# Rotary embedding, bf16 inside and f32 outside: smaller transfers with loads and stores taking turns in the software DMA queue

## The chip, the cores and the metric

The kernel runs on one core of a Trainium2 chip. Times are device microseconds (us) of one launch, as the median of several runs. "Span" is the length of one profiled execution; the time of the launch is a little above it.

## The reference

```python
# x: (8, 8, 1024, 64) f32; freqs: (32,) f32; positions: (1024,) int
angles = np.outer(positions, freqs)
cos, sin = np.cos(angles), np.sin(angles)
x_first, x_second = x[..., :32], x[..., 32:]
out_first  = x_first * cos - x_second * sin
out_second = x_first * sin + x_second * cos
```

16.78 MB are read and 16.78 MB written, both in f32. Each element takes part in three operations of the vector engine (DVE), which is little for so much data.

## The kernel before

A tile is 128 partitions, each with C = 64 positions of one head: 64 x 64 f32, a run of 16 KB in memory. Eight tiles cover x. All eight loads are issued by POOL (the GpSimd engine) at the start. They cast f32 to bf16 on the way, so a tile holds 8 KB per partition; the stores cast back (the packet records of this kernel hold 1024 load packets of 8 KB and 1024 store packets of 16 KB). ("Software queue" is below the queue that POOL fills, q0 software_dynamic in the page's rows; SP fills q1 and ACT q10, both hardware_dynamic.)

```python
C = 64; chunks = seq // C; group = P // chunks; ntiles = bh // group; run = C * d
pos_i = singles.tile([P, C, 1], positions.dtype)
for g in range(group):                       # 8 small DMAs on SP and ACT in turn
    eng = nc.sync if g % 2 == 0 else nc.scalar
    eng.dma_start(out=pos_i[g * chunks:(g + 1) * chunks],
                  in_=bass.AP(tensor=positions.tensor, offset=positions.offset,
                              ap=[[C, chunks], [1, C], [1, 1]]))
fr = singles.tile([P, half], f32)
nc.scalar.dma_start(out=fr, in_=freqs[None, :].to_broadcast([P, half]))
for g in range(ntiles):                      # all loads first
    xt = xpool.tile([P, C, d], bf16)
    nc.gpsimd.dma_start(out=xt.rearrange("p c d -> p (c d)"), in_=hbm(x, g))
    xts.append(xt)
# ... cut: tables sin_h, cos_h of [P, C, half] in bf16, by three DVE passes and three on ACT ...
for g in range(ntiles):
    # ... cut: views xf, xs of xt and of, os_ of ot; temporaries t1, t2 ...
    v.tensor_mul(out=t1, in0=xf, in1=sin_h)
    v.tensor_mul(out=t2, in0=xs, in1=sin_h)
    v.tensor_mul(out=of, in0=xf, in1=cos_h)
    v.tensor_mul(out=os_, in0=xs, in1=cos_h)
    v.tensor_sub(out=of, in0=of, in1=t2)
    v.tensor_add(out=os_, in0=os_, in1=t1)
    nc.gpsimd.dma_start(out=hbm(out, g), in_=ot.rearrange("p c d -> p (c d)"))
```

Of the kernel before, what the change touches and what calls it, by code (L numbers as in the profile page):

```python
# [2 lines left out]

# [4 lines left out]


@with_exitstack  # L10
def kernel(
    ctx: ExitStack,
    tc: tile.TileContext,
    x: bass.AP,
    freqs: bass.AP,
    positions: bass.AP,
    out: bass.AP,
):
    nc = tc.nc
    f32 = mybir.dt.float32  # L20
    bf16 = mybir.dt.bfloat16
    Sin = mybir.ActivationFunctionType.Sin
    Alu = mybir.AluOpType

    b, h, seq, d = x.shape
    bh = b * h
    half = d // 2
    P = 128
    twopi = 2 * math.pi


    C = 64
    chunks = seq // C
    group = P // chunks
    ntiles = bh // group
    run = C * d
    assert chunks * C == seq and group * chunks == P and ntiles * group == bh

    singles = ctx.enter_context(tc.tile_pool(name="singles", bufs=1))
    xpool = ctx.enter_context(tc.tile_pool(name="xin", bufs=ntiles))  # L40
    opool = ctx.enter_context(tc.tile_pool(name="xout", bufs=ntiles))
    tpool = ctx.enter_context(tc.tile_pool(name="tmp", bufs=2))

    def hbm(t, g):
        return bass.AP(tensor=t.tensor, offset=t.offset + g * P * run, ap=[[run, P], [1, run]])


    pos_i = singles.tile([P, C, 1], positions.dtype)
    for g in range(group):
        eng = nc.sync if g % 2 == 0 else nc.scalar  # L50
        eng.dma_start(
            out=pos_i[g * chunks:(g + 1) * chunks],
            in_=bass.AP(tensor=positions.tensor, offset=positions.offset,
                        ap=[[C, chunks], [1, C], [1, 1]]))
    fr = singles.tile([P, half], f32)
    nc.scalar.dma_start(out=fr, in_=freqs[None, :].to_broadcast([P, half]))


    xts = []
    for g in range(ntiles):  # L60
        xt = xpool.tile([P, C, d], bf16)
        nc.gpsimd.dma_start(out=xt.rearrange("p c d -> p (c d)"), in_=hbm(x, g))  # L62
        xts.append(xt)


    half_pi = singles.tile([P, 1], f32)
    nc.vector.memset(half_pi, math.pi / 2)  # L67
    pos_f = singles.tile([P, C, 1], f32)
    nc.vector.tensor_copy(out=pos_f, in_=pos_i.bitcast(mybir.dt.int32)[:, :, :1])  # L69
    fturn = singles.tile([P, 1, half], f32)  # L70
    nc.vector.tensor_scalar_mul(out=fturn[:, 0, :], in0=fr, scalar1=1.0 / twopi)  # L71
    turns = singles.tile([P, C, half], f32)
    nc.vector.tensor_mul(out=turns, in0=pos_f.to_broadcast([P, C, half]),  # L73
                         in1=fturn.to_broadcast([P, C, half]))
    whole = singles.tile([P, C, half], f32)
    magic = 1.5 * 2.0 ** 23
    nc.vector.tensor_scalar(out=whole, in0=turns, scalar1=magic, scalar2=magic,  # L77
                            op0=Alu.add, op1=Alu.subtract)
    nc.vector.tensor_sub(out=turns, in0=turns, in1=whole)  # L79
    sin_h = singles.tile([P, C, half], bf16)  # L80
    cos_h = singles.tile([P, C, half], bf16)
    nc.scalar.activation(out=sin_h, in_=turns, func=Sin, scale=twopi)  # L82

    nc.scalar.activation(out=whole, in_=turns, func=mybir.ActivationFunctionType.Abs)  # L84
    nc.scalar.activation(out=cos_h, in_=whole, func=Sin, scale=-twopi, bias=half_pi)  # L85

    v = nc.vector
    for g in range(ntiles):
        xt = xts[g]
        xf = xt[:, :, :half]  # L90
        xs = xt[:, :, half:]
        ot = opool.tile([P, C, d], bf16)
        of = ot[:, :, :half]
        os_ = ot[:, :, half:]
        t1 = tpool.tile([P, C, half], bf16)
        t2 = tpool.tile([P, C, half], bf16)
        v.tensor_mul(out=t1, in0=xf, in1=sin_h)  # L97
        v.tensor_mul(out=t2, in0=xs, in1=sin_h)  # L98
        v.tensor_mul(out=of, in0=xf, in1=cos_h)  # L99
        v.tensor_mul(out=os_, in0=xs, in1=cos_h)  # L100
        v.tensor_sub(out=of, in0=of, in1=t2)  # L101
        v.tensor_add(out=os_, in0=os_, in1=t1)  # L102
        nc.gpsimd.dma_start(out=hbm(out, g), in_=ot.rearrange("p c d -> p (c d)"))  # L103


# [1 line left out]
_INS = ['x', 'freqs', 'positions']  # L107
_OUTS = [((8, 8, 1024, 64), 'float32')]


# [23 lines left out]
```

## Time and profile before

| | before |
|---|---|
| time, median | 87.09 us (87.08 to 87.15) |
| span | 85.5 us |
| DVE busy | 60.8 us (71%) |
| POOL busy | 8.8 us (10%) |
| software DMAs | 16, of 2 MB of f32 each |
| last landing (semaphore records) | 83.8 us |

The prediction below reads the DMA rows, the stretches and the timeline of this profile. Two more views follow. First the page's queue rows: packets, MB and the time of the packets as a share of 16 engines' span.

```profile
q0 software_dynamic: 2304, 25.17, 96.4%
q10 hardware_dynamic: 272, 0.05, 0.4%
q1 hardware_dynamic: 128, 0.03, 0.3%
```

2304 packets are 16 DMAs x (128 data packets + 16 semaphore packets, whose records are of 4 bytes). Then one microsecond near the end (start and end, length, busy time of DVE, ACT and POOL, clock, DMA share, GB/s):

```profile
77.00:78.00 1.00, 0.00 (x0) 0.00 (x0) 0.53 (x1) 1.00 0.71 279
```

279 GB/s instead of some 430: by the packet records the median DMA engine had nothing to do from 77.97 to 78.43 us, just before the first packets of the last store, which waited for DVE (done at 76.97). The slowest DMA engine was busy with earlier data until 78.37, though, and all had begun the last store by 78.52, so DVE was holding the end itself by only some 0.15 us. Last, what the SP engine waited for, which shows the end of the program: after its wait for the last store it waits twice more until all engines are ready to leave, 1.0 us together (0.8 is the longer of the two, here the second).

```profile
SPq L129 <- DMA out_dram<-ot: 81.3, 1, 81.3
SPq L129 <- PEq L129: 1.0, 2, 0.8
```

### The profile page before, as it was taken

Reading aid. Unit: us, or ns where it says so; the run is one execution under the profiler, and the core shown is the slowest. Engines: PE = TensorE matmul, PEld = TensorE weight load, DVE = VectorE, ACT = ScalarE, POOL = GpSimd, SP = SyncE. Lnnn points to the kernel's source line nnn. Section 1 sums busy time; section 2 is a strip of 40 time slices with the busy share of each in tenths; the row PEclk is TensorE's granted clock in tenths of the full one; section 3 lists DMA queues with packets and bytes.
Section 4 is the critical chain, followed back from the end, with each engine's and each line's share of the span. In section 5 each row is a group of like instructions: output and inputs, shape, how many; then the busy total and the mean of one; then the engine's idle time right before and its main releaser. Section 6 shows DMA issues by size and latency. Waiting matters only on the chain.

```text
span 85.5 us, 146 instructions
## 1 busy us (share of the span) xinstructions
DVE 60.8 (71%) x54; ACT 7.0 (8%) x4; POOL 8.8 (10%) x20
## 2 busy tenths in 40 slices
DVE  0000002995599999999999999999999999990000
ACT  0500000004992000000000000000000000000000
POOL 5960000000000011020020020020020002002000
DMA  0799979999999999999999999999999999999990
GB/s 8 81 225 208 184 140 231 203 226 203 226 203 226 211 218 215 215 222 207 222 326 460 399 475 391 475 391 475 383 475 391 468 391 468 391 468 368 376 368 0
DMA packets 2704, 25.25 MB, mean 295 GB/s; under 512 B 528, under 2 KB 656, under 8 KB 656
## 3 DMA queue, kind: packets, MB, share of 16 engines
q0 software_dynamic: 2304, 25.17, 96.4%
q10 hardware_dynamic: 272, 0.05, 0.4%
q1 hardware_dynamic: 128, 0.03, 0.3%
HBM read 16.86 MB, written 16.78 MB: 393 GB/s over the span
## 4 chain that ended last, share of the span: by engine, by line
issue 75%; DMA 10%; POOL 4%; POOLq 1%; PEldq 0%
DMA xt<-in_x_dram 10%; POOL out_dram L103 4%; POOLq L129 1%; POOLq L103 0%; PEldq L129 0%
## 5 line engine op out<-in xcount | busy, mean ns | idle before, releaser
L103 POOL DMA_DIRECT2D out_dram<-ot x8 | 4.3, 533 | 67.9 <-DVE ot L102 67.9
L97 DVE TENSOR_TENSOR t<-xt,sin_h 128x2048 bf16<-128x2048 bf16 x8 | 9.8, 1228 | 2.0 <-ACT sin_h L82 2.0
L102 DVE TENSOR_TENSOR ot<-ot,t 128x2048 bf16<-128x2048 bf16 x8 | 9.8, 1231 | 0.0
L100 DVE TENSOR_TENSOR ot<-xt,cos_h 128x2048 bf16<-128x2048 bf16 x8 | 9.8, 1230 | 0.0
L101 DVE TENSOR_TENSOR ot<-ot,t 128x2048 bf16<-128x2048 bf16 x8 | 9.8, 1229 | 0.0
L98 DVE TENSOR_TENSOR t<-xt,sin_h 128x2048 bf16<-128x2048 bf16 x8 | 9.8, 1228 | 0.0
L99 DVE TENSOR_TENSOR ot<-xt,cos_h 128x2048 bf16<-128x2048 bf16 x8 | 9.8, 1228 | 0.0
L69 DVE CAST pos_f<-pos_i 128x64 f32<-128x64 int32 x1 | 0.2, 196 | 7.7 <-DMA pos_i<-in_positions_dram 7.7
L62 POOL DMA_DIRECT2D xt<-in_x_dram x8 | 4.4, 579 | 0.8 <-PEq L129 0.8
L71 DVE TENSOR_SCALAR fturn<-fr 128x32 f32<-128x32 f32 x1 | 0.2, 181 | 5.5 <-DMA fr<-in_freqs_dram 5.5
L82 ACT ACTIVATE sin_h<-turns 128x2048 bf16<-128x2048 f32 x1 | 1.9, 1909 | 16.1 <-DVE turns L79 16.1
L79 DVE TENSOR_TENSOR turns<-turns,whole 128x2048 f32<-128x2048 f32 x1 | 2.3, 2293 | 0.0
L73 DVE TENSOR_TENSOR turns<-pos_f,fturn 128x2048 f32<-128x2048 f32 x1 | 2.3, 2293 | 0.0
L85 ACT ACTIVATE cos_h<-whole,half_pi 128x2048 bf16<-128x2048 f32 x1 | 2.0, 2002 | 0.0
L84 ACT ACTIVATE whole<-turns 128x2048 f32<-128x2048 f32 x1 | 1.9, 1893 | 0.0
L82 ACT ACT_TABLE_LOAD x1 | 1.3, 1283 | 3.1 <-DMA pos_i<-in_positions_dram 3.1
L77 DVE TENSOR_SCALAR whole<-turns 128x2048 f32<-128x2048 f32 x1 | 1.2, 1227 | 0.0
L67 DVE MEMSET half_pi<- 128x1 f32 x1 | 0.1, 59 | 0.8 <-PEq L118 0.8
L118 POOL MEMSET const-float32-0.0<- 128x1 f32 x1 | 0.1, 99 | 0.2 <-issue 0.2
L118 POOL MEMSET const-bfloat16-1.0<- 128x1 bf16 x1 | 0.1, 102 | 0.0
L118 POOL MEMSET const-float32-1.0<- 128x1 f32 x1 | 0.1, 99 | 0.0
L118 POOL MEMSET const-uint8-127<- 128x1 uint8 x1 | 0.1, 99 | 0.0
## 6 DMA issues: line engine op xcount, KB each, us to landing
out_dram<-ot POOLq DMA_DIRECT2D x8, 2048.0 KB, 13.2
xt<-in_x_dram POOLq DMA_DIRECT2D x8, 1024.0 KB, 24.4
pos_i<-in_positions_dram ACTq DMA_DIRECT2D x4, 8.0 KB, 3.2
pos_i<-in_positions_dram SPq DMA_DIRECT2D x4, 8.0 KB, 2.9
fr<-in_freqs_dram ACTq DMA_DIRECT2D x1, 16.0 KB, 11.7
```

What stands on the lines that cost most here:

```text
L62: nc.gpsimd.dma_start(out=xt.rearrange("p c d -> p (c d)"), in_=hbm(x, g))
L73: nc.vector.tensor_mul(out=turns, in0=pos_f.to_broadcast([P, C, half]), in1=fturn.to_broadcast([P, C, half]))
L79: nc.vector.tensor_sub(out=turns, in0=turns, in1=whole)
L82: nc.scalar.activation(out=sin_h, in_=turns, func=Sin, scale=twopi)
L85: nc.scalar.activation(out=cos_h, in_=whole, func=Sin, scale=-twopi, bias=half_pi)
L97: v.tensor_mul(out=t1, in0=xf, in1=sin_h)
L98: v.tensor_mul(out=t2, in0=xs, in1=sin_h)
L99: v.tensor_mul(out=of, in0=xf, in1=cos_h)
L100: v.tensor_mul(out=os_, in0=xs, in1=cos_h)
L101: v.tensor_sub(out=of, in0=of, in1=t2)
L102: v.tensor_add(out=os_, in0=os_, in1=t1)
L103: nc.gpsimd.dma_start(out=hbm(out, g), in_=ot.rearrange("p c d -> p (c d)"))
```

## The change

Its intent: a casting load reads 4 bytes for 2 written, a casting store the reverse; if they take turns in the queue, the reads of the one might overlap the writes of the other. For that the transfers are cut to 512 KB with runs of 4 KB (C = 16; K = 4 of them make a group of 128 x 2048 products, so DVE's instructions keep their size), only three groups are loaded ahead, and from then on each store is followed by a load. The tables shrink to a quarter, the positions come in one DMA, and the frequencies are thereby first in ACT's queue.

```diff
-    C = 64
+    C = 16
+    K = 4
+    ahead = 3
...
-    for g in range(group):
-        eng = nc.sync if g % 2 == 0 else nc.scalar
-        eng.dma_start(out=pos_i[g * chunks:(g + 1) * chunks],
-            in_=bass.AP(..., ap=[[C, chunks], [1, C], [1, 1]]))
+    nc.sync.dma_start(out=pos_i,
+        in_=bass.AP(..., ap=[[0, group], [C, chunks], [1, C]]))
...
-    for g in range(ntiles):
-        xt = xpool.tile([P, C, d], bf16)
-        nc.gpsimd.dma_start(out=xt.rearrange("p c d -> p (c d)"), in_=hbm(x, g))
+    def load(g, k):
+        nc.gpsimd.dma_start(out=xts[g][:, k].rearrange("p c d -> p (c d)"), in_=hbm(x, g * K + k))
+    for g in range(ahead):
+        for k in range(K):
+            load(g, k)
...   (the same six DVE operations, on [P, K, C, half], tables broadcast over K)
-        nc.gpsimd.dma_start(out=hbm(out, g), in_=ot.rearrange("p c d -> p (c d)"))
+        for k in range(K):
+            nc.gpsimd.dma_start(out=hbm(out, g * K + k), in_=ot[:, k].rearrange("p c d -> p (c d)"))
+            if g + ahead < ngroups:
+                load(g + ahead, k)
```

More of the change, by code (lines that the diff above doesn't have):

```diff
@@ L29, with hbm @@
     twopi = 2 * math.pi
-    C = 64
+    C = 16
+    K = 4
     chunks = seq // C
     group = P // chunks
-    ntiles = bh // group
     run = C * d
-    assert chunks * C == seq and group * chunks == P and ntiles * group == bh
+    ngroups = bh // (group * K)
+    ahead = 3
+    assert chunks * C == seq and group * chunks == P and ngroups * group * K == bh
     singles = ctx.enter_context(tc.tile_pool(name="singles", bufs=1))
-    xpool = ctx.enter_context(tc.tile_pool(name="xin", bufs=ntiles))
-    opool = ctx.enter_context(tc.tile_pool(name="xout", bufs=ntiles))
+    xpool = ctx.enter_context(tc.tile_pool(name="xin", bufs=ngroups))
+    opool = ctx.enter_context(tc.tile_pool(name="xout", bufs=ngroups))
     tpool = ctx.enter_context(tc.tile_pool(name="tmp", bufs=2))
-    def hbm(t, g):
-        return bass.AP(tensor=t.tensor, offset=t.offset + g * P * run, ap=[[run, P], [1, run]])
+    def hbm(t, n):
+        return bass.AP(tensor=t.tensor, offset=t.offset + n * P * run, ap=[[run, P], [1, run]])
     pos_i = singles.tile([P, C, 1], positions.dtype)
-    for g in range(group):
-        eng = nc.sync if g % 2 == 0 else nc.scalar
-        eng.dma_start(
-            out=pos_i[g * chunks:(g + 1) * chunks],
-            in_=bass.AP(tensor=positions.tensor, offset=positions.offset,
-                        ap=[[C, chunks], [1, C], [1, 1]]))
+    nc.sync.dma_start(
+        out=pos_i,
+        in_=bass.AP(tensor=positions.tensor, offset=positions.offset,
+                    ap=[[0, group], [C, chunks], [1, C]]))
     fr = singles.tile([P, half], f32)
     nc.scalar.dma_start(out=fr, in_=freqs[None, :].to_broadcast([P, half]))
-    xts = []
-    for g in range(ntiles):
-        xt = xpool.tile([P, C, d], bf16)
-        nc.gpsimd.dma_start(out=xt.rearrange("p c d -> p (c d)"), in_=hbm(x, g))
-        xts.append(xt)
+    xts = [xpool.tile([P, K, C, d], bf16, name="xt") for _ in range(ngroups)]
+    def load(g, k):
[3 more added lines that the diff above has]
+            load(g, k)
     half_pi = singles.tile([P, 1], f32)
@@ L87 @@
     v = nc.vector
-    for g in range(ntiles):
+    sin_b = sin_h[:, None].to_broadcast([P, K, C, half])
+    cos_b = cos_h[:, None].to_broadcast([P, K, C, half])
+    for g in range(ngroups):
         xt = xts[g]
-        xf = xt[:, :, :half]
-        xs = xt[:, :, half:]
-        ot = opool.tile([P, C, d], bf16)
-        of = ot[:, :, :half]
-        os_ = ot[:, :, half:]
-        t1 = tpool.tile([P, C, half], bf16)
-        t2 = tpool.tile([P, C, half], bf16)
-        v.tensor_mul(out=t1, in0=xf, in1=sin_h)
-        v.tensor_mul(out=t2, in0=xs, in1=sin_h)
-        v.tensor_mul(out=of, in0=xf, in1=cos_h)
-        v.tensor_mul(out=os_, in0=xs, in1=cos_h)
+        xf = xt[:, :, :, :half]
+        xs = xt[:, :, :, half:]
+        ot = opool.tile([P, K, C, d], bf16)
+        of = ot[:, :, :, :half]
+        os_ = ot[:, :, :, half:]
+        t1 = tpool.tile([P, K, C, half], bf16)
+        t2 = tpool.tile([P, K, C, half], bf16)
+        v.tensor_mul(out=t1, in0=xf, in1=sin_b)
+        v.tensor_mul(out=t2, in0=xs, in1=sin_b)
+        v.tensor_mul(out=of, in0=xf, in1=cos_b)
+        v.tensor_mul(out=os_, in0=xs, in1=cos_b)
         v.tensor_sub(out=of, in0=of, in1=t2)
         v.tensor_add(out=os_, in0=os_, in1=t1)
-        nc.gpsimd.dma_start(out=hbm(out, g), in_=ot.rearrange("p c d -> p (c d)"))
+        for k in range(K):
+            nc.gpsimd.dma_start(out=hbm(out, g * K + k), in_=ot[:, k].rearrange("p c d -> p (c d)"))
+            if g + ahead < ngroups:
+                load(g + ahead, k)
 _INS = ['x', 'freqs', 'positions']
```

## The prediction

- A packet of 4 KB was put at 154.1 ns, so a DMA of 512 KB at 1.254 us. The kernel after bore this out: its load packets start 154 ns apart and its store packets 153, and such a DMA takes 1.255 us among loads and 1.244 among stores. The 21 ns of a semaphore packet are from the kernel before (21 ns from its start to the next load packet).
- The table passes came to 2.9 us with 0.69 for each product, 0.42 for the scalar pass and 0.65 for the sine. The kernel after took 0.69, 0.43, 0.69 and 0.63, and 2.8 in all.
- The positions were put on two DMA engines, with 64 packets of 128 bytes on each; the kernel after has 128 such packets in two chains, and 2 semaphore packets.

With these terms the main sum came to 91.9 us, 88.2 to the last packet and 3.7 from there to the end of the launch, and the weighing of all cases to 90.0. That an engine has two halves which might run on their own is the first rival's supposition; no trace here shows such halves.

> **What bounds the kernel now.** I read the page's DMA rows first, because the kernel does little arithmetic on much data, then the stretches by stage, then the order of the instructions.
>
> ```profile
> DMA  0799979999999999999999999999999999999990
> GB/s 8 81 225 208 184 140 231 203 226 203 226 203 226 211 218 215 215 222 207 222 326 460 399 475 391 475 391 475 383 475 391 468 391 468 391 468 368 376 368 0
> HBM read 16.86 MB, written 16.78 MB: 393 GB/s over the span
> ```
>
> The DMA engines are full from slice 2 to slice 38. The GB/s row seems to say that loads run at half the speed of stores, but it counts a casting load by its bf16 side; on the f32 side both phases move the same. The stretches (start and end in us, length, busy time of DVE, ACT and POOL, clock, DMA share, GB/s) make that exact:
>
> ```profile
> 9.00:13.00 4.00, 0.00 (x0) 0.00 (x0) 0.00 (x0) 1.00 0.86 164
> 14.00:42.00 28.00, 25.61 (x22) 5.71 (x3) 1.08 (x2) 1.00 1.03 216
> 46.00:76.00 30.00, 30.00 (x28) 0.00 (x0) 2.13 (x4) 1.00 1.06 430
> ```
>
> Loads 2 x 216 = 432 GB/s of f32, stores 430. 33.55 MB at 431 GB/s are 77.8 us; the first packet goes out at about 2.6 us, some 2 us are lost in the start and in the dip at 9 to 13 us, and the end comes at about 83.5. That is the whole span of 85.5 less its tail: **the DMA engines are the bound**. But a second limit lies close beside it:
>
> ```profile
> 8.60 0.20 DVE L69 CAST pos_f<-pos_i 128x64 f32<-128x64 int32 x1 [7.73 <-DMA pos_i<-in_positions_dram]
> 14.31 0.18 DVE L71 TENSOR_SCALAR fturn<-fr 128x32 f32<-128x32 f32 x1 [5.52 <-DMA fr<-in_freqs_dram]
> 14.53 2.29 DVE L73 TENSOR_TENSOR turns<-pos_f,fturn 128x2048 f32<-128x2048 f32 x1
> ...
> 20.44 1.91 ACT L82 ACTIVATE sin_h<-turns 128x2048 bf16<-128x2048 f32 x1 [16.09 <-DVE turns L79]
> ...
> 22.38 1.22 DVE L97 TENSOR_TENSOR t<-xt,sin_h 128x2048 bf16<-128x2048 bf16 x1 [1.98 <-ACT sin_h L82]
> ```
>
> DVE waits for the frequencies until 14.31, builds the tables until 22.38, then never stops. The eighth store is issued at 77.27 (its line is in the timeline) and takes 6.5 us to land, at 83.8. The seven stores ahead of it, queued behind the loads, are through at about the same time. So DVE alone would end the kernel no earlier either; a faster end needs both an earlier DVE and more bytes per us from the DMA engines.
>
> [...] the records of single load packets start 606 ns apart and last 624. [...] The kernel before has 16 chunks in front, and its queue q1 carries four such DMAs in 128 packets, 4 x (16 data + 16 semaphore): all engines. [...]
>
> **The change part by part.**
> *Bytes*: the same. *Packets*: 16 KB become 4 KB of f32, [...] and 64 DMAs instead of 16, each with a semaphore packet of 21 ns per engine. One DMA of 512 KB gives each engine 8 packets: 8 x 154.1 + 21 = 1.254 us. 64 of them are 80.2 us against 16 x (8 x 606 + about 10) = 77.7 us before: **2.5 us more DMA work**.
> *Issue*: 64 DMAs x 0.55 us (before: 579 and 533 ns each) are 35 us on POOL, below the 1.25 us that each transfer takes. Hidden.
> *Tables*: a quarter as large. On the path from positions to the first product: cast 0.2, fturn 0.18, 0.69 + 0.42 + 0.69 for the three DVE passes, sine about 0.65 [...]: 2.9 us, where the same work took 8.1 us (14.31 to 22.38). 5 us less.
> *Frequencies*: now the first DMA on ACT's queue, issued near 0.74 rather than 2.60, in front of the flood of loads; they should land by 3 us instead of 14.3.
> *Positions*: one DMA whose source leads with a zero stride of 2. [...] They start at about 1.75 us; some 29 go at about 30 ns before the first load packets appear at 2.6. I reckon the other 35 alternate with load packets, each at 154 ns plus 30 to 200 ns for the small one (the dip at 9 to 13 us, where five or so frequency packets per engine cost about 1 us, says 200; the position packets before it cost about 40). After a first load packet of about 1 us: positions at 10 to 17 us, say 11.5.
> *DVE*: six products and sums of 1.13 us a group as before, 6.8 us. [...]
> *The queue*: only 12 loads (three groups) are ahead. They end at 2.6 + 12 x 1.254 = 17.7 us. The thirteenth transfer is the first store, and it needs: positions 11.5, 0.15 hop, 2.9 tables, 6.8 first group, 0.35 hop to POOL, and 1.35 from issue to first packet (as 1.25 to 2.6 for the first load): 23.0. **So the DMA engines stand idle for about 5 us.** From there 52 DMAs x 1.254 = 65.2 us: 88.2. Groups 1 and 2 are then ready for DVE, each later group's load arrives 10 us after the last while DVE needs 6.8, so DVE is not the bound. The tail (last packet at about 83.5 to 85.5) is 2.1 us and the time is 1.6 us above the span: 88.2 + 3.7 = 91.9 us. With positions at 10 us it is 90.4; at 5 us, where the first four loads and not the tables hold the first group, about 87.
>
> **Rivals.**
> *Read and write overlap.* A casting load reads 4 bytes and writes 2, a casting store the reverse. If both halves of an engine really ran on their own, a load and a store together would take 6 units instead of 8, and the 40 mixed DMAs 12.5 us less; DVE would then be the bound, from 14.5 us: 8 x 6.8 = 54.5, then the last four stores 0.35 + 1.35 + 5.0, tail 3.7: about 80 us. This is surely what the change is for. [...] Against it: load and store packets have nearly the same period (606, 605 ns), packets overlap by only 18 ns among loads and 37 among stores, and at the one turn from loads to stores the first store gains only 20 ns. [...] I give a large gain 0.2, a partial one (84 to 87 us) 0.1.
> *The positions come early* (all 16 engines, or the two engines get through before the loads): no idle DMA, about 87 us, the same as before. 0.15.
> *The positions come later still*, each packet costing 200 ns: 17 us, and about 96 us. 0.1.
> *DVE or POOL becomes the bound*, [...] the stores before took 0.53 us of POOL beside a busy DVE, so I see no sign of it; eight DMAs would have to take over 10 us a group.
>
> **Range and chances.** The serial sum gives 88.5 to 94 with the centre near 91.5, the early positions 87, overlap 80 to 86. The median of these is about 90.0 us; 82 to 94.5 should hold it 8 times in 10. Faster than 85.35: 0.25; within 2%: 0.2; above 88.83: 0.55.
>
> **What would show it.** Right: the two queues' rows with 64 packets per engine on two engines only for the positions, their landing after 9 us, a gap in the DMA row between about 18 and 23 us, the mixed phase at one load and one store per 2.5 us (about 315 GB/s as counted), DVE waiting for loads from the fourth group on. Wrong: mixed phase nearer 400 GB/s as counted, with the end set by DVE's last store; or positions landed by 5 us and no gap. If the 4 KB packets are slower than 154 ns, the mixed rate falls below 315 and all is later by that.

## The result, and the profile after

The kernel after took 90.07 us (89.95 to 90.22, 3 runs) against 87.09: a ratio of 1.034 (interval 1.032 to 1.037).

| | before | after |
|---|---|---|
| time, median | 87.09 us | 90.07 us |
| span | 85.5 us | 88.4 us |
| first product on DVE | 22.4 us | 10.2 us |
| first packet of x to last landing | 81.1 us | 82.4 us |
| last landing | 83.8 us | 85.1 us |
| last landing to end of span | 1.75 us | 3.39 us |
| time less span, of the profiled run | 1.8 us | 1.8 us |

The 2.9 us of span have two parts: **the last byte lands 1.3 us later, and 1.6 us more pass after it**. The DMA rows of the page after:

```profile
DMA  0799999999999999999999999999999999999900
GB/s 2 80 184 208 208 211 208 210 208 209 208 331 424 354 363 402 319 308 303 303 308 321 330 327 321 312 302 305 308 311 325 374 419 424 422 422 417 396 19 0
...
q0 software_dynamic: 9216, 25.17, 108.0%
q1 hardware_dynamic: 130, 0.02, 0.1%
q10 hardware_dynamic: 144, 0.02, 0.1%
```

There is no gap from the third slice to the 38th. (The share over 100% is no extra speed: it adds up the packets' own durations, and packets overlap. A load packet lasts 173 ns where the next starts after 154, a store packet 191 where it starts after 153; these overlaps of 19 and 38 ns are those of the 16 KB packets before, 18 and 37.) The stretches of the three stages, loads only, mixed, stores only:

```profile
8.00:24.00 16.00, 13.78 (x13) 1.22 (x2) 6.82 (x13) 1.00 1.12 209
28.00:64.00 36.00, 27.20 (x25) 0.00 (x0) 15.45 (x29) 1.00 1.19 326
72.00:82.00 10.00, 5.07 (x5) 0.00 (x0) 2.10 (x4) 1.00 1.25 422
```

The GB/s column counts the bf16 side of a load. Whether the mixed stage is faster has to be asked in packets, since every data packet is 4 KB of f32. An engine moves 6.38 packets per us in the first stretch, 6.40 in the second and 6.43 in the third. The second holds 45% loads and 55% stores; at the rates of the pure stages it would have 6.41. **Taking turns gains nothing.**

The head of the timeline after shows why there is no gap, in three of its lines:

```profile
5.14 0.17 DVE L73 CAST pos_f<-pos_i 128x16 f32<-128x16 int32 x1 [4.27 <-DMA pos_i<-in_positions_dram]
5.22 0.17 DVE L75 TENSOR_SCALAR fturn<-fr 128x32 f32<-128x32 f32 x1
...
10.22 1.23 DVE L103 TENSOR_TENSOR t<-xt,sin_h 128x2048 bf16<-128x2048 bf16 x1 [2.91 <-DMA xt<-in_x_dram]
```

The positions are there at 5.1 us, not at 8.6, and the frequencies at 4.6 (from the semaphore records), not at 14.3. The first group begins at 10.2 us, having waited last for its own data, and the first store is issued at 18.2. Moreover the compiled order is not the order of the source: the scheduler of the framework put 17 loads, not 12, ahead of the first store, then four stores, a load, three stores, a load, and strict turns only after that.

Waits on POOL, new in this kernel:

```profile
POOL xt L63 <- DMA xt<-in_x_dram: 14.3, 21, 1.0
POOL out_dram L110 <- DMA out_dram<-ot: 12.8, 16, 1.0
...
POOL out_dram L110 <- DMA xt<-in_x_dram: 5.9, 9, 1.0
```

By the semaphore records the program's software DMAs report their landings on eight semaphores in turn, and from the ninth on each one is issued only after the landing of the one eight places before it (the ninth at 6.67 us, the first having landed at 6.38). That looks alarming, and the chain of waits is made of it ("DMA xt<-in_x_dram 61%"), but in the mixed stage seven or eight transfers of 1.25 us are always under way or queued, and the engines don't run dry (under 0.1 us idle after the first microseconds). The wait is a symptom of full DMA engines.

And the end of the program, again as SP's own waits:

```profile
SPq L138 <- DMA out_dram<-ot: 83.5, 4, 79.9
SPq L138 <- PEq L138: 3.0, 2, 2.6
```

Where SP stood 1.0 us in its two waits between the last store and the exit, it now stands 3.0; it is the first of the two that has grown, from 0.2 to 2.6. The instruction records say who is late: POOL's last drain ends 0.70 us after the last landing in the kernel before, and 2.66 us after it in this one. Of these 1.96 us, 0.3 are given back behind the drain, where the kernel before had one more late instruction on DVE.

### The profile page after: what moved, and what is told of

The parts are those of the page before. It is cut to its first block, busy times and chain, and to the rows that moved or that the text cites. A ratio compares the mean times of both kernels' runs of the same rounds, so it can differ in the third digit from the quotient of the medians. Undisturbed runs are those within 1.5% of the kernel's fastest.

```text
span 88.4 us, 195 instructions
## 1 busy us (share of the span) xinstructions
DVE 57.1 (65%) x54; ACT 3.2 (4%) x4; POOL 34.4 (39%) x68
## 4 chain that ended last, share of the span: by engine, by line
DMA 72%; DVE 7%; issue 6%; POOL 3%; DVEq 1%; POOLq 1%; PEldq 0%
DMA xt<-in_x_dram 61%; DMA out_dram<-ot 11%; POOL out_dram L110 2%; DVE t L103 1%; DVEq L138 1%; DVE ot L105 1%; DVE ot L107 1%; DVE t L104 1%; DVE ot L106 1%; POOL xt L63 1%; POOLq L138 1%; PEldq L138 0%; POOLq L110 0%
## 5 line engine op out<-in xcount | busy, mean ns | idle before, releaser
L110 POOL DMA_DIRECT2D out_dram<-ot x32 | 17.0, 533 | 27.6 <-DMA out_dram<-ot 12.8
L63 POOL DMA_DIRECT2D xt<-in_x_dram x32 | 17.2, 544 | 17.2 <-DMA xt<-in_x_dram 14.3
L86 ACT ACTIVATE sin_h<-turns 128x512 bf16<-128x512 f32 x1 | 0.6, 631 | 4.9 <-DVE turns L83 4.9
L89 ACT ACTIVATE cos_h<-whole,half_pi 128x512 bf16<-128x512 f32 x1 | 0.7, 722 | 0.0
L83 DVE TENSOR_TENSOR turns<-turns,whole 128x512 f32<-128x512 f32 x1 | 0.7, 693 | 0.0
L77 DVE TENSOR_TENSOR turns<-pos_f,fturn 128x512 f32<-128x512 f32 x1 | 0.7, 691 | 0.0
L88 ACT ACTIVATE whole<-turns 128x512 f32<-128x512 f32 x1 | 0.6, 614 | 0.0
```

The lines of the kernel that those rows point to most:

```text
L63: nc.gpsimd.dma_start(out=xts[g][:, k].rearrange("p c d -> p (c d)"), in_=hbm(x, g * K + k))
L77: nc.vector.tensor_mul(out=turns, in0=pos_f.to_broadcast([P, C, half]), in1=fturn.to_broadcast([P, C, half]))
L83: nc.vector.tensor_sub(out=turns, in0=turns, in1=whole)
L86: nc.scalar.activation(out=sin_h, in_=turns, func=Sin, scale=twopi)
L110: nc.gpsimd.dma_start(out=hbm(out, g * K + k), in_=ot[:, k].rearrange("p c d -> p (c d)"))
```

## The experiments

**Theory after reading the traces.** The time is (a) the packets' own time on engines that move one after the other, whatever their order, plus (b) what the start loses, plus (c) a drain of POOL that grows with the number of software DMAs. Rivals: the turns between loads and stores cost or save something; the drain grows with the number of packets; the start of the kernel after saved nothing. Seven kernels were run, in two batches; the kernel before took 87.23 us (86.99 to 87.61) beside the first and 87.19 (87.05 to 87.30) beside the second. All gave correct results.

| run | software DMAs | packets | last landing | landing to end of POOL's drain | time | ratio to before |
|---|---|---|---|---|---|---|
| before | 16 | 16 KB | 83.76 | 0.70 | 87.09 | 1 |
| after | 64 | 4 KB | 85.06 | 2.66 | 90.07 | 1.034 |
| e1_head | 16 | 16 KB | 82.85 | 0.70 | 86.41 | 0.990 |
| e2_loads_first | 64 | 4 KB | 84.78 | 2.66 | 90.13 | 1.033 |
| e3_16_dmas | 16 | 4 KB | 84.33 | 0.70 | 88.01 | 1.009 |
| e5_8k_runs | 32 | 8 KB | 84.53 | 1.35 | 87.87 | 1.008 |
| e6_64_dmas_16k | 64 | 16 KB | 84.21 | 2.66 | 89.37 | 1.025 |
| e7_first_plain | 15 | 16 KB | 82.85 | 0.66 | 86.41 | 0.992 |
| e8_last_plain | 14 | 16 KB | 83.09 | done before | 86.14 | 0.990 |

(Landings in us from the span's start, from the semaphore records; times are medians.)

### e1_head: the head of the change alone

```diff
-    for g in range(group):          # kernel before: eight small position DMAs
-        ...
+    nc.sync.dma_start(out=pos_i, in_=bass.AP(..., ap=[[0, group], [C, chunks], [1, C]]))
```

> Kernel before with the head of the change alone: positions in one DMA, so that the frequencies' DMA is first on ACT's queue; 16 KB packets and all loads first as before. Theory (time = DMA packet work + what the start and the tail lose): the dip at 9 to 13 us, where tiny frequency packets run between the loads, goes away, the last landing moves from 83.8 us to about 82.5, the tail of 1.7 us after it stays, the time is about 85.9 us (1.4% faster). Rival (the 1.2 us of the dip are not what the kernel after saved at its start; the packets are cheaper than reckoned): no change, 87.1 us.

Measured: last landing 82.85 us, 0.9 earlier; the span 1.3 us shorter, 84.2; the time 86.41 us, a ratio of 0.990 (0.987 to 0.993). The stretch of the former dip, in this kernel:

```profile
9.00:13.00 4.00, 2.19 (x1) 1.77 (x1) 0.00 (x0) 1.00 1.06 221
```

221 GB/s where the prediction's view of the kernel before had 164: over 4 us this is 0.23 MB of bf16, or 1.1 us of loading. DVE ends at 67.8 us instead of 77.0, so the idle half microsecond at 78 is gone too. The expected 85.9 us was missed by 0.5: the landing came 0.35 later than expected, the tail was 0.3 shorter (1.4 us), and the time lies 2.2 us above the span here, against 1.8 before; e3, e7 and e8 share this, the kernels with 32 or 64 DMAs don't. What these 0.4 us are, the traces don't show, since they lie outside the span.

### e2_loads_first: the alternation alone undone

```diff
-    ahead = 3
+    ahead = ngroups
```

> Kernel after with the alternation alone undone: the same 64 DMAs of 4 KB packets, all 32 loads first. Theory (alternation is worth nothing and costs nothing; an engine moves one packet after the other in either order): last landing 85.1 us, tail 3.4 us, time 90.1 us, within 0.5%. Rival 1 (read and write sides overlap a little at each turn, so the alternation saved something): slower, 91 us or more. Rival 2 (turns between loads and stores cost time): faster, 89 us or less.

Measured: 90.13 us against 90.07 of the kernel after; last landing 84.78 against 85.06. Both rivals fall. The stretches of its loads and of its stores are those of the kernel after:

```profile
8.00:40.00 32.00, 30.06 (x27) 0.95 (x2) 13.35 (x26) 1.00 1.12 209
46.00:82.00 36.00, 18.53 (x17) 0.00 (x0) 12.75 (x24) 1.00 1.24 420
```

So the order of loads and stores in the queue is worth nothing either way, within the 0.3 us of landing that separate the two. (That much is scatter: the execution profiled here took 89.94 us, the shortest of four, and that of the kernel after 90.22, the longest of three.)

### e3_16_dmas: the same packets, a quarter of the DMAs

```diff
-        nc.gpsimd.dma_start(out=xts[g][:, k]..., in_=hbm(x, g * K + k))
+        if k == 0:      # one DMA of 128 x K x 1024 elements; hbm4 has ap=[[run, P], [P * run, K], [1, run]]
+            nc.gpsimd.dma_start(out=xts[g].rearrange("p k c d -> p k (c d)"), in_=hbm4(x, g))
         (the stores likewise)
```

> Kernel after with the four loads and the four stores of a group in one DMA each: the same 8192 packets of 4 KB, but 16 DMAs instead of 64. Packet work 16 x (32 x 154.1 + 21) = 79.2 us against 80.2, so last landing about 84.0 us. Theory (the longer tail, 3.4 us from the last landing to the end against 1.7 before, comes from the number of DMAs that POOL issued): tail 1.7 us, time about 87.4 us. Rival (it comes from the number of packets): tail 3.4 us, time about 89.0 us.

Measured: 88.01 us, 2.1 below the kernel after, with the same 8192 data packets, as its queue row shows (8448 less 16 x 16 semaphore packets):

```profile
q0 software_dynamic: 8448, 25.17, 110.5%
```

The drain is back at 0.70 us, and SP's two waits with it, at 1.0 us:

```profile
SPq L144 <- PEq L144: 1.0, 2, 0.6
```

The rival (the drain follows the packets) falls. (The 154.1 ns of the expectation are what the kernel after shows: 154 between load packets, 153 between store packets.) The last landing came 0.7 us earlier than in the kernel after, where 48 semaphore packets fewer per engine, of 21 ns each, are 1.0 us. The time missed its 87.4 by 0.6, for the landing, 0.3 later than expected, and the 0.4 us named under e1; the tail, 1.4 us, was again 0.3 shorter.

### e5_8k_runs: between the two

```diff
-    C = 16
-    K = 4
+    C = 32
+    K = 2
```

> Kernel after with 8 KB runs (C = 32, K = 2): 32 DMAs of 1 MB, 8 packets per engine each. Packet work 32 x (8 x 304.7 + 21) = 78.7 us, so last landing about 83.5 us (85.1 less 1.5). The tail lies between those of 16 and of 64 DMAs, about 2.3 us, by either theory of the tail; time about 87.5 us. If the packet term were wrong (a fixed cost per DMA or none at all), the last landing would stay at 85 or drop to 82.5.

(The 304.7 ns of the expectation are an estimate, on the line through 154.1 ns at 4 KB and 606 at 16 KB.) Measured: 87.87 us. The drain took 1.35 us, on the line through 16 and 64 DMAs (0.70 and 2.66). The last landing, 84.53, came 1.0 us later than expected. Two holes account for it in the page's GB/s row, whose 13th slice (near 27 us) is 172 and whose 37th (near 79 us) is 375: in the second the DMA engines wait for DVE's last group, as in the kernel before. In the first they don't stand idle: about 25 load packets between 26.8 and 28.3 us last 0.4 to 0.9 us instead of 0.32, and why isn't shown. The profiled execution was also the longest of the four, 88.37 us against 87.72 to 87.94, so about half of the missing 1.0 us may be its own. So this run supports (c) but is a poor measure of (a).

### e6_64_dmas_16k: many DMAs, large packets

```diff
 # on the kernel of e1_head
-        nc.gpsimd.dma_start(out=xt.rearrange("p c d -> p (c d)"), in_=hbm(x, g))
+        for q in range(4):
+            nc.gpsimd.dma_start(out=xt[32 * q:32 * (q + 1)].rearrange("p c d -> p (c d)"),
+                                in_=hbm(x, g)[32 * q:32 * (q + 1)])
         (the stores likewise)
```

> The kernel of e1_head with each of its 16 transfers cut into four DMAs of 32 partitions: the same 2048 packets of 16 KB, but 64 DMAs. So far the time between the last landing and the end of POOL's last drain was 0.70 us with 16 DMAs (three kernels, 2048 or 8192 packets), 1.35 with 32 and 2.66 with 64 (two kernels). Theory (each software DMA costs 0.041 us in that drain): 2.66 us here, 3.4 us from the last landing to the end, last landing about 83.9 us for 48 more rounds of semaphore packets (48 x 21 ns), time about 89.2 us. Rival (the drain follows the packets of 4 KB): 0.70 us, time about 87.2 us. If 32 partitions at a time are slower by themselves, the last landing shows it, not the drain.

Measured: 89.37 us, last landing 84.21, drain 2.66 us. The data packets are those of e1_head, 2048 (3072 less 64 x 16 of semaphores):

```profile
q0 software_dynamic: 3072, 25.17, 94.8%
```

SP's waits are nonetheless those of the kernel after:

```profile
SPq L129 <- PEq L129: 3.0, 2, 2.6
```

This settles the drain: 16, 32 and 64 software DMAs give 0.70, 1.35 and 2.66 us, whatever the packets, which is 0.041 us for each DMA. It also prices the cutting alone: e6 less e1 is 3.0 us for 48 more DMAs and not one data packet more, of which 2.0 are the drain and 1.4 the landing (48 semaphore packets of 21 ns, 1.0 us, are most of that), less the 0.4 outside the span.

### e7_first_plain and e8_last_plain: attempts to beat both

```diff
 # e7, on the kernel of e1_head: first tile f32, loaded on ACT's queue
+        if g == 0:
+            xt = singles.tile([P, C, d], f32)
+            nc.scalar.dma_start(out=xt.rearrange("p c d -> p (c d)"), in_=hbm(x, g))
 # e8, on e7: last tile f32, stored on SP's queue
+        last = g == ntiles - 1
+        ot = (singles if last else opool).tile([P, C, d], f32 if last else bf16)
-        nc.gpsimd.dma_start(out=hbm(out, g), ...)
+        (nc.sync if last else nc.gpsimd).dma_start(out=hbm(out, g), ...)
```

> An attempt to beat both: the kernel of e1_head with the first of its eight loads as a plain f32 DMA on ACT's queue, in front of POOL's. Theory: the first load packet goes out at about 2.0 us instead of 2.7, DMA work stays, so the last landing comes 0.5 to 0.7 us earlier, at about 82.2; DVE spends some 4.3 us more on the f32 tile (four products at 2.3 us instead of 1.2) but has 10 us to spare; time about 85.8 us. Rival (two queues that take turns on an engine cost more than the earlier start brings): 86.4 us or more.

Measured: 86.41 us, no gain. ACT issued the load by 1.59 us, yet its first packet went out at 2.81, no earlier than POOL's first in e1_head (2.73). The expectation of 2.0 us was wrong: an earlier issue brought no earlier first packet. Why isn't shown: the frequencies' packets, which run from 1.73 to 3.95 us, stand ahead of it in the same queue, and no run tried the load without them.

> The kernel of e7_first_plain with the last of its eight stores plain too (f32 tile, on SP's queue), so that POOL's drain of the software queue can run while the last store is under way. Theory: the 0.7 us of the drain after the last landing go, DVE needs 4.5 us more (ends near 76.5, just before the DMA engines reach the last store at about 77), time about 85.2 us, over 2% below the kernel before. Rival (DVE becomes late, the DMA engines wait for its last tile): 86 us or more.

Measured: 86.14 us (86.14 to 86.60). POOL's drain now ends at 78.6 us, under the last store, and the time from the last landing to the end of the span falls from 1.4 to 0.9 us, as meant; half of it is lost again because the landing comes 0.24 us later, DVE having ended at 76.7. The plain store took 6.4 us from issue to landing; the last casting store of the kernel before took 6.5. It is a ratio of 0.990 (0.987 to 0.993): with e1_head the fastest, 1% below the kernel before and 4% below the kernel after. Between e1 and e8 the ratios don't decide.

## Why the prediction was right or wrong

**Right in direction; the number is luck.** 90.0 us were predicted, 90.07 measured. But the number came out of a weighing of several cases, and its main sum, 91.9 us, was wrong in three places that partly cancelled: the idle time, the start and the tail. What happened to the positions is the prediction's own rival "The positions come early", given 0.15 and "about 87 us, the same as before"; "positions landed by 5 us and no gap" stands among its signs of being wrong. For that case it was 3 us too low, since it had neither the lost start nor the longer tail. Three of its signs of being right did appear: two DMA engines for the positions, the mixed phase near 315 GB/s as counted (326), and DVE waiting for loads, though one group later than it said (2.7 to 3.1 us before each group from the fifth on).

*Packet work: right.* "2.5 us more DMA work." In the time from the first packet to the last landing less what stood idle after the first microseconds (from the packet records: 1.3 us in the kernel before, under 0.1 after), the kernel before has 79.8 us and the kernel after 82.4: 2.6 us. The measured 6.38 and 6.43 packets per us are 1.255 and 1.244 us for a DMA of 8 packets; the estimate was 1.254.

*No overlap of reads and writes: right.* The rival given 0.2 is refuted by the mixed stage of the kernel after (6.40 packets per us and engine, where the pure stages would give 6.41), and by e2 (90.13 us without the turns, 90.07 with them). The reading of the trace that spoke against it, load and store packets of nearly the same period (606 and 605 ns) that overlap by only 18 and 37 ns, fits this but isn't proved by it: loads and stores alike move 4 bytes of f32 per element at the memory's side, and no run separates a limit there from one in the DMA engines. Finer turns than 32 KB per engine weren't tried.

*Positions: the step that failed.* The prediction put them on two engines, and that was right: q1's 130 packets are 128 of data, in two chains, and 2 semaphores. But "35 alternate with load packets, each at 154 ns plus 30 to 200 ns for the small one" was wrong. The records show each engine's 64 packets of 128 bytes 9.4 ns apart in two bursts, 32 before its first load packets and 32 after, instead of one by one. They landed at 5.1 us, not at 11.5.

*"So the DMA engines stand idle for about 5 us": failed with it.* There was no idle time. Even apart from the positions it would have been shorter, since 17 loads and not 12 stood ahead of the first store in the compiled order, which can't be read off the source.

*The start: left out of the sum.* The main sum let loads run at full rate from 2.6 us. In the record the first load packets of the kernel after last up to 1.1 us each, and 1.9 us are lost between the first packet and full rate (82.1 us from first to last packet, less the 80.2 of work in the forecast; at the measured 1.244 to 1.255 us for a DMA, 64 of them are 79.6 to 80.3).

*The tail: left unchanged, and wrong.* "The tail (last packet at about 83.5 to 85.5) is 2.1 us" was carried over from the kernel before. It became 3.7 us (84.7 to 88.4). The four-fold number of DMAs was priced in issue time on POOL (35 us reckoned, 34.2 measured and hidden, right) but not in the drain, 2.66 us instead of 0.70, which nothing hides. e3 and e6 show that it follows the number of DMAs; at 2.0 us it is the largest single term of the loss.

Together: 91.9, less 5.3 of idle that didn't come, plus 1.9 of start, plus 1.6 of tail, plus 0.2 for the time above the span, is 90.3. (The prediction's 1.6 us above the span is the median of the timed launches less the span of the profiled one, which itself took 87.28: 1.8 us.)

The loss of 3.0 us by the experiments: the head alone gains 0.8 (e1 against before), 4 KB packets cost 1.6 (e3 against e1, which also has the larger tables and all loads first), 64 DMAs instead of 16 cost 2.1 (after against e3), the alternation 0 (e2). The sum is 2.9.

## What to carry to other kernels

Here the DMA engines were full nearly from end to end, and reordering the transfers was worth nothing (90.13 against 90.07 us); larger packets (1.6 us), less idle time (0.8, by the head of e1) and fewer software DMAs (2.1) were what paid. Cutting transfers had a price after the last byte, not only per byte: 0.041 us of drain for each software DMA. So count software DMAs in the tail, and put several runs into one DMA if small runs are needed (e3, 2.1 us below the kernel after). And small loads that a table depends on belong in front of the bulk loads: that part of the change alone, in e1, was 1% faster than the kernel before (ratio 0.990).
